# The last two down chunks of the first MLP as one pair, with four of sixteen k tiles in seven products

## The chip, the cores and the metric

The kernel runs on one core of a Trainium2 chip. The metric is the device time of one execution in microseconds, the median of several runs. All times below that are positions ("at 1293") are microseconds from the start of the profiled execution's span.

The core has five engines that work side by side: TensorE (PE; its weight loads are listed as PEld), VectorE (DVE), ScalarE (ACT), GpSimd (POOL) and SyncE (SP). SP computes nothing here; it issues most of the DMA transfers. Each engine works through its own instruction stream in the order that was fixed when the program was built, and waits on semaphores of the others.

## The reference

A decoder trunk of two layers over 256 positions of width 2048, in float32. Each layer is a token mixer (a gated MLP with spatial gating in layer 0, an S5 state-space layer with a gated linear unit in layer 1), then cross-attention to a memory of 256 rows, then a squared-ReLU MLP, each behind an RMSNorm and added to the residual `x`. What matters here is the MLP:

```
def squared_relu_mlp(h, w_up, w_down):
    return jnp.square(jax.nn.relu(h @ w_up)) @ w_down
...
x = x + squared_relu_mlp(rms_norm(x, g_ff[i]), f_w_up[i], f_w_down[i])
```

with `w_up` 2048 x 8192 and `w_down` 8192 x 2048.

## The kernel before

**Arithmetic.** TensorE works on `F32R` operands. Every operand is split into a high part (ACT casts it to F32R) and a low part (DVE subtracts the high part from the raw value): `split`, L103 and L104. A product is then three matmuls: activation high and low with weight high, and activation high with weight low. A weight tile is 512 KB, two k tiles of 128 rows by 512 columns. `wload` loads it on SP into a ring of four raw buffers (`wraw`; the first MLP has a fifth), `wtile` splits it into `whi` and `wlo`, rings of three.

**The first MLP** (`mlp`, layer 0) runs over four blocks `b` of 2048 hidden features. In each block the up products come first: four chunks `n` of 512 features, each as two `gemm_feat` calls, whose results are squared-ReLUed (`r`) and split into `hh` and `hl`. Then come the down products: four chunks `n` of 512 output columns, each a `gemm_hid` of eight weight tiles with 12 matmuls each (two row tiles `t`, two k tiles, three matmuls), added into `x` by `gather` (L688, scaled with the squared norm factor `r2`). In the last block, chunk `n` of `x` is then final, and one tick after it (a tick is one weight tile) `nxt.chunk(x, n)` makes the next layer's activation of it: sums of squares on ACT, eight transposes on TensorE, and high and low parts on ACT (L245) and DVE (L246). The next layer is the S5 mixer, whose first products take the activation's k tiles in order.

**Activations** live in the pool `act` with two slots of 32 KB per partition, tag "act". During the first MLP one slot holds the MLP's own input `hT`, the other the tile `room` of `ssm_prep`. The next activation (`nxt.start()`, `n_b.act` here) takes a slot that is free by then. A tile that takes a slot waits until everything that used the tile before it there has ended.

**`ssm_prep`** prepares the S5 layer's tables beside the first MLP. Its steps are queued in `side` and one is traced at every second tick, at a priority 200 instructions later than its place. It works on small tiles out of `room` and copies them to DRAM on POOL's queue: `Qd`, `Pd` and `Kd`. The last of these copies are four of `Kd` (`respond`, L1191).

**`gemm_seven`** is used by both attentions (values and output projection) and by most of the second MLP, and not by the first MLP. It makes two chunks of 512 columns at once, for both row tiles. For the first k tiles it replaces the eight block products of the 2 x 2 x 2 block scheme by seven, in Strassen's manner: some products take sums of activation blocks (`sums`, made by `token_sums` in four additions and a split, L720 to L723) and differences of raw weight tiles (`run`, L821, L827, L834, L841). Each of the seven is 6 matmuls with its own split of its weights. Four raw tiles are loaded for this by `fetch` (L764) into tiles that `ws()` returns, outside the weight ring. The other weight tiles go through `direct`, 12 matmuls each as in `gemm_hid`, and lie between the products:

```
summed((0, 1), 0, run, t1)
block((1, 0), 0, 0, raw[0, 0], far.get((0, 0)))
m5, m1 = keep((0, 1), 0), keep((1, 0), 1)
block((0, 0), 0, 1, raw[1, 0], far.get((1, 0)))
whole(1, 1)
```

`keep` copies a partial result from PSUM to SBUF (ACT, L812); `gather` then adds it to `x`. With `ahead=None` four of the 16 k tiles go this way; with `ahead`, in the second MLP, eight.

Of the kernel before, what the change touches and what calls it, by code (L numbers as in the profile page):

```python
# [9 lines left out]
F32 = mybir.dt.float32  # L10
F32R = mybir.dt.float32r
# [5 lines left out]
P = 128  # L17
D = 2048
S = 256
KT = D // P  # L20
NB = 512
NCH = D // NB
KB = 2
# [6 lines left out]
DFF = 4 * D  # L30
# [8 lines left out]
class Trunk:  # L39
# [604 lines left out]
    def mlp(self, x, layer, cur, nxt):  # L644
        nc, a, tc = self.nc, self.a, self.tc
        wu, wd = a["f_w_up"][layer], a["f_w_down"][layer]
        hT = cur.act
        with tc.tile_pool(name="ml", bufs=4, reuse_waits="tile") as mp:
            r2 = mp.tile([P, 32 if layer else 24], F32, name="r2", bufs=1)[:, 0:2]
            ws = lambda: mp.tile([P, KB * NB], F32, name="ws", bufs=4)  # L650
            run = lambda: mp.tile([P, KB * NB], F32, name="run", bufs=1)
            kept = lambda i: more[:, 6 + i // 2, i % 2 * NB:i % 2 * NB + NB]
            self.fifth = None if nxt.closing else mp
            for b in range(DFF // D):
                hid = []
                for n in range(NCH):
                    h = mp.tile([P, 4, S], F32R, name="hh")
                    l = mp.tile([P, 4, S], F32R, name="hl")
                    rs = []
                    for i in range(2):  # L660
                        r = mp.tile([P, 2, S], F32, name="r", bufs=2)
                        self.gemm_feat(hT, wu, 2 * (NCH * b + n) + i, r)
                        nc.vector.scalar_tensor_tensor(out=r, in0=r, scalar=0.0, in1=r, op0=ALU.max, op1=ALU.mult)
                        self.split(h[:, 2 * i:2 * i + 2], l[:, 2 * i:2 * i + 2], r)
                        rs.append(r)
                    hid.append((h, l))
                    if nxt.closing and n == 0:
                        sums = []
                    if nxt.closing and n < 2:
                        sums.append(self.token_sums(ws(), lambda: mp.tile([P, 4, 2, P], F32R, name="sums", bufs=4), *rs))  # L670
                    if nxt.closing and n == NCH - 2:
                        more = self.act.tile([P, 8, KB * NB], F32, name="more", tag="act")
                        ahead = [self.block_ahead(more, wd, 2 * j, b * KT, j) for j in range(1 if b == DFF // D - 1 else 2)]
                        ahead[0][-2]()
                if nxt.closing:
                    ahead[0][-1](0, 1, 2)
                if nxt.closing:
                    own = lambda: mp.tile([P, KB * NB], F32R, name="own", bufs=2)
                    nxt.room = lambda: mp.tile([P, 2, NB], F32, name="g", tag="ws", bufs=4)
                if b == 0:  # L680
                    rstd = cur.rstd()
                    nc.vector.tensor_tensor(out=r2, in0=rstd, in1=rstd, op=ALU.mult)
                if b == DFF // D - 1 and not nxt.closing:
                    nxt.start()

                def gather(t, n, part, cs=None):
                    xc = x[:, t, cs or slice(n * NB, (n + 1) * NB)]
                    nc.vector.scalar_tensor_tensor(out=xc, in0=part, scalar=r2[:, t:t + 1], in1=xc,  # L688
                                                   op0=ALU.mult, op1=ALU.add)

                for n in range(NCH):
                    end = b == DFF // D - 1
                    if nxt.closing and not (end and n >= NCH - 2):
                        if n % 2 == 0:
                            self.gemm_seven((ws, run, kept), lambda kt, t: [f[:, kt % 4, t * P:(t + 1) * P]
                                                                            for f in hid[kt // 4]],
                                            sums, wd, n, b * KT, gather, own=own, ahead=ahead[n // 2],
                                            then=ahead[1] if n == 0 and len(ahead) > 1 else None)
                            if end:
                                nxt.start()  # L700
                    elif nxt.closing and end and n == NCH - 1:
                        self.gemm_last(hid, wd, n, b * KT, lambda t, acc: nxt.finish(x, t, lambda cs: gather(
                            t, n, acc[:, cs.start - n * NB:cs.stop - n * NB], cs)))
                        break
                    else:
                        acc = self.gemm_hid(hid, wd, n, b * KT)
                        for t in range(2):
                            gather(t, n, acc[:, t, :])
                    if end:
                        self.at(4 + n if nxt.closing and n < 2 else 1, lambda n=n: nxt.chunk(x, n))  # L710

            self.fifth = None

# [255 lines left out]
    def ssm_prep(self, pool):  # L969
# [28 lines left out]
        def home(n):  # L998
            used[0] += n
            return room[:, used[0] - n:used[0]]  # L1000

        bbs = [home(4 * 2 * 16).rearrange("p (g k c) -> p g k c", g=4, k=2) for _ in range(4)]
        qts = [home((T + 1) * 4 * 16).rearrange("p (w g c) -> p w g c", g=4, c=16) for _ in range(4)]
        pos = [home(4 * 2 * 64).rearrange("p (t r s) -> p t r s", t=4, r=2) for _ in range(4)]
        kds = [home(NL * 2 * 16).rearrange("p (w i c) -> p w i c", i=2, c=16) for _ in range(2)]

        def cmul(orr, oi, ar, ai, br, bi):
            t1 = pool.tile(W, F32, name="cm_1", tag="w4")[:, 0:ar.shape[1]]
            t2 = pool.tile(W, F32, name="cm_2", tag="w6")[:, 0:ar.shape[1]]
            v.tensor_tensor(out=t1, in0=ar, in1=br, op=ALU.mult)  # L1010
            v.tensor_tensor(out=t2, in0=ai, in1=bi, op=ALU.mult)
            v.tensor_tensor(out=orr, in0=t1, in1=t2, op=ALU.subtract)
            v.tensor_tensor(out=t1, in0=ar, in1=bi, op=ALU.mult)
            v.tensor_tensor(out=t2, in0=ai, in1=br, op=ALU.mult)
            v.tensor_tensor(out=oi, in0=t1, in1=t2, op=ALU.add)
# [41 lines left out]
        def zoh():  # L1057
            lr, li = e["lr"], e["li"]
            pr, pi = e["pw"][1]
            fr, fi = pool.tile(W, F32, name="fr", tag="w2"), pool.tile(W, F32, name="fi", tag="w3")  # L1060
            nr, den = pool.tile(W, F32, name="nr", tag="w7"), pool.tile(W, F32, name="den", tag="w9")
            v.tensor_tensor(out=den, in0=lr, in1=lr, op=ALU.mult)
            v.tensor_tensor(out=nr, in0=li, in1=li, op=ALU.mult)
            v.tensor_tensor(out=den, in0=den, in1=nr, op=ALU.add)
            v.reciprocal(out=den, in_=den)
            v.tensor_scalar(out=nr, in0=pr, scalar1=-1.0, scalar2=None, op0=ALU.add)
            v.tensor_scalar(out=li, in0=li, scalar1=-1.0, scalar2=None, op0=ALU.mult)
            cmul(fr, fi, nr, pi, lr, li)
            v.tensor_tensor(out=fr, in0=fr, in1=den, op=ALU.mult)
            v.tensor_tensor(out=fi, in0=fi, in1=den, op=ALU.mult)  # L1070
            pt = self.ps([P, 4, P])
            for k, t in enumerate((fr, fi)):
                nc.tensor.transpose(pt[:, k, :], t, self.ident)
            nc.scalar.copy(out=F, in_=pt[:, 0:2, :])
            e["f"] = fr[:, 0:64], fi[:, 0:64]
            lk = pool.tile([P, 2, 64], F32, name="lk")
            for k in range(2):
                nc.scalar.copy(out=lk[:, k], in_=e["f"][k])
            nc.gpsimd.dma_start(out=Ld[0], in_=lk)
            row(1)  # L1080

        def row(k):
            lk = pool.tile([P, 2, 64], F32, name="lk")
            cmul(lk[:, 0], lk[:, 1], *(f[:, 0:64] for f in e["pw"][k]), *e["f"])
            nc.gpsimd.dma_start(out=Ld[k], in_=lk)

        def power(k):
            h = k // 2
            cmul(*place(k), *e["pw"][h], *e["pw"][k - h])
            if k < T:  # L1090
                row(k)
# [542 lines left out]
```

## Time and profile before

| | us |
|---|---|
| median of 3 runs (2771.16 to 2774.17) | 2772.53 |
| the profiled execution's own time | 2768.95 |
| its span | 2767.2 |
| last block of the first MLP, down products | 1293.6 to 1384.1 |

The span goes from the first to the last instruction. Busy times of engines are the page's first part; stretches of the span can be asked for one by one, with the busy time of each engine in them. A row of a timeline gives the start, the duration, the engine, the line of the kernel, the operation, what it writes and reads, and how many were merged; in brackets stand the idle time before it and what ended it. In a row of a group, `x46` is a count, and three numbers with strokes are minimum, median and maximum in ns. DMA rows have the size and the microseconds from issue to landing.

### The profile page before, as it was taken

The numbers are of one execution on the slowest core, as the hardware profiler recorded it, in microseconds if no ns is written. First come the engines' busy times: TensorE is split into PE (matmuls) and PEld (weight loads), VectorE is DVE, ScalarE is ACT, GpSimd is POOL, SyncE is SP. The second block draws the span as 40 slices with busy tenths as digits, with TensorE's granted clock in tenths as the row PEclk, the third lists the DMA queues.
The fourth block names the chain that finished last, engine by engine and source line by source line (L and its number), as shares of the span: only waits on it lengthen the run. The fifth ranks groups of instructions, "written<-read, shape, count | busy, mean of one in ns | idle before, by whom it ended". The sixth has DMA issues, their size and how long they took to land. (4 is left out here: it accounts for less than half of the span.)

```text
span 2767.2 us, 39486 instructions
## 1 busy us (share of the span) xinstructions
PE 2747.1 (99%) x14978; PEld 2326.5 (84%) x14978; DVE 2046.0 (74%) x2809; ACT 1421.1 (51%) x1814; POOL 186.7 (7%) x331
## 2 busy tenths in 40 slices
PE   9999999999999999999999999999999999999998
PEld 7888888888888888888888888888888888888887
DVE  6865756778888878787577667557767978869685
ACT  6545544555544434444566445445555655546454
POOL 0100000001011111111203100000000000000000
PEclk9999999999999999999999999999999999999999
DMA  8766665557788888886879767565557557475565
GB/s 298 231 196 230 202 183 181 170 159 231 220 281 258 262 258 256 266 256 221 235 238 288 214 202 231 182 195 153 182 163 232 176 174 244 153 248 163 177 212 159
DMA packets 194175, 593.75 MB, mean 215 GB/s; under 512 B 44096, under 2 KB 45168, under 8 KB 193472
## 3 DMA queue, kind: packets, MB, share of 16 engines
q1 hardware_dynamic: 153456, 537.46, 61.3%
q0 software_dynamic: 40000, 52.71, 6.8%
q8 instruction: 117, 1.92, 0.3%
q10 hardware_dynamic: 528, 1.06, 0.1%
q14 instruction: 74, 0.61, 0.1%
HBM read 567.51 MB, written 23.46 MB: 214 GB/s over the span
## 5 line engine op out<-in xcount | busy, mean ns | idle before, releaser
L104 DVE TENSOR_TENSOR wlo<-wraw,whi 128x1024 fp32r<-128x1024 f32 (+1 forms) x865 | 1051.3, 1221 | 444.5 <-ACT whi L103 438.2
L103 ACT CAST whi<-wraw 128x1024 fp32r<-128x1024 f32 (+1 forms) x865 | 909.2, 1053 | 812.2 <-PE acc L875 181.2
L174 PE MATMUL acc<-act,whi 128*128 128x512 f32 x3072 | 740.9, 391 | 0.6 <-DVE act L246 0.6
L174 PEld LDWEIGHTS acc<-act,whi 128*128 128x128 f32 x3072 | 563.1, 188 | 110.7 <-issue 1.4
L179 PEld LDWEIGHTS acc<-act,wlo 128*128 128x128 f32 x3072 | 395.0, 191 | 17.0 <-DVE wlo L104 1.4
L179 PE MATMUL acc<-act,wlo 128*128 128x256 f32 x3072 | 403.2, 283 | 1.2 <-DVE wlo L104 0.8
L159 PE MATMUL acc<-whi,act 128*128 128x512 f32 x1472 | 369.4, 393 | 5.4 <-ACT whi L103 5.4
L159 PEld LDWEIGHTS acc<-whi,act 128*128 128x128 f32 x1472 | 274.8, 189 | 62.6 <-ACT whi L103 5.6
L776 PE MATMUL acc<-whi,act 128*128 128x512 f32 x864 | 233.0, 392 | 0.1
L875 PE MATMUL acc<-whi,hl 128*128 128x512 f32 x544 | 212.7, 391 | 0.0
L874 PE MATMUL acc<-whi,hh 128*128 128x512 f32 x544 | 212.6, 391 | 0.0
L159 PE MATMUL acc<-wlo,act 128*128 128x512 f32 x736 | 197.2, 389 | 0.0
L776 PEld LDWEIGHTS acc<-whi,act 128*128 128x128 f32 x864 | 160.3, 188 | 36.8 <-ACT ends L812 1.9
L159 PEld LDWEIGHTS acc<-wlo,act 128*128 128x128 f32 x736 | 138.3, 188 | 28.9
L877 PE MATMUL acc<-wlo,hh 128*128 128x512 f32 x544 | 145.8, 389 | 0.0
L776 PE MATMUL acc<-wlo,act 128*128 128x512 f32 x432 | 133.1, 390 | 0.0
L190 ACT COPY r<-acc 128x512 f32<-128x512 f32 x64 | 37.7, 589 | 162.9 <-PE acc L174 162.8
L875 PEld LDWEIGHTS acc<-whi,hl 128*128 128x128 f32 x544 | 102.1, 188 | 22.2 <-issue 1.0
L776 PE MATMUL acc<-whi,hh 128*128 128x512 f32 x308 | 120.5, 391 | 0.0
L874 PEld LDWEIGHTS acc<-whi,hh 128*128 128x128 f32 x544 | 102.1, 188 | 21.4 <-issue 0.2
L877 PEld LDWEIGHTS acc<-wlo,hh 128*128 128x128 f32 x544 | 102.0, 188 | 21.4 <-issue 0.2
L776 PE MATMUL acc<-whi,hl 128*128 128x512 f32 x308 | 119.9, 389 | 0.0
(373 smaller groups left out, 2883.5 us busy)
## 6 DMA issues: line engine op xcount, KB each, us to landing
wraw<-in_f_w_up SPq DMA_DIRECT2D x256, 512.0 KB, 4.4
wraw<-in_f_w_down SPq DMA_DIRECT2D x200, 512.0 KB, 5.0
wraw<-in_x_w_q SPq DMA_DIRECT2D x64, 512.0 KB, 4.3
wraw<-in_x_w_k SPq DMA_DIRECT2D x64, 512.0 KB, 4.4
wraw<-in_b_w_out SPq DMA_DIRECT2D x64, 512.0 KB, 4.5
wraw<-in_a_w_in SPq DMA_DIRECT2D x63, 512.0 KB, 4.5
wraw<-in_x_w_v SPq DMA_DIRECT2D x48, 512.0 KB, 4.4
wraw<-in_x_w_o SPq DMA_DIRECT2D x48, 512.0 KB, 4.4
```

Of the source, the lines that this page charges most:

```text
L103: self.nc.scalar.copy(out=hi, in_=src)
L104: return self.nc.vector.tensor_tensor(out=lo, in0=src, in1=hi.bitcast(F32), op=ALU.subtract).ins
L159: nc.tensor.matmul(out[t], a[:, kt, sl], b[:, kk, :], start=st and a is ah, stop=en)
L174: nc.tensor.matmul(acc[:, f, :], hi[:, kk, sl], both[:, kt].rearrange("p a s -> p (a s)"), start=first and kk == 0, stop=last and kk == FK ...
L179: nc.tensor.matmul(acc[:, f, 0:S], lo[:, kk, sl], ah[:, kt, :], start=False, stop=last and kk == FK - 1, skip_group_check=True)
L190: nc.scalar.copy(out=dst, in_=acc[:, :, S:])
L776: mm = lambda s, m, e: nc.tensor.matmul(out, s, m, start=key not in begun, stop=e, skip_group_check=True)
L874: nc.tensor.matmul(acc[:, t, :], ah, hi[:, kk, :], start=kt == 0, stop=False)
L875: nc.tensor.matmul(acc[:, t, :], al, hi[:, kk, :], start=False, stop=False)
L877: nc.tensor.matmul(acc[:, t, :], hid[kt // 4][0][:, kt % 4, sl], lo[:, kk, :], start=False, stop=kt == KT - 1)
```

## The change

In the last block of the first MLP the down chunks n = 2 and n = 3 are made by one call of `gemm_seven` without `ahead`: four of the 16 k tiles in seven products, twelve directly. The token sums that it needs come from the up products of chunk 0 of that block. Their intermediate result is written to a new part of `room` (`self.spare`), their high and low parts to two new tiles `sums`. The four raw weight tiles, the differences (`run`) and the kept results lie in a tile `more`, which is taken from the pool `act` behind the last up products and ahead of the next activation. Chunk 3 of the next activation is planned one tick after chunk 2, both behind the pair. The tile `lk` of `ssm_prep` shares its slot with the tiles of tag `w9`.

```diff
-            ws = lambda: mp.tile([P, KB * NB], F32, name="ws", bufs=4)
-            run = lambda: mp.tile([P, KB * NB], F32, name="run", bufs=1)
+            if nxt.closing:
+                ws = lambda: mp.tile([P, KB * NB], F32, name="ws", bufs=4)
+                run = lambda: mp.tile([P, KB * NB], F32, name="run", bufs=1)
+            else:
+                ws, run = lambda: next(homes), lambda: more[:, 4]
...
-                    if nxt.closing and n == 0:
+                    if n == 0:
                         sums = []
-                    if nxt.closing and n < 2:
-                        sums.append(self.token_sums(ws(), lambda: mp.tile([P, 4, 2, P], F32R, name="sums", bufs=4), *rs))
+                    if nxt.closing and n < 2 or not nxt.closing and n == 0 and b == DFF // D - 1:
+                        sums.append(self.token_sums(ws() if nxt.closing else self.spare, lambda: mp.tile([P, 4, 2, P], F32R, name="sums", bufs=4 if nxt.closing else 2),
+                                                    *rs))
...
                 if b == DFF // D - 1 and not nxt.closing:
+                    more = self.act.tile([P, 8, KB * NB], F32, name="more", tag="act")
+                    homes = iter([more[:, k] for k in range(4)])
                     nxt.start()
...
+                    elif end and n >= NCH - 2 and not nxt.closing:
+                        if n % 2 == 0:
+                            self.gemm_seven((ws, run, kept), lambda kt, t: [f[:, kt % 4, t * P:(t + 1) * P]
+                                                                            for f in hid[kt // 4]],
+                                            sums, wd, n, b * KT, gather)
                     else:
                         acc = self.gemm_hid(hid, wd, n, b * KT)
...
                     if end:
-                        self.at(4 + n if nxt.closing and n < 2 else 1, lambda n=n: nxt.chunk(x, n))
+                        self.at(4 + n if nxt.closing and n < 2 else 1 if n < 3 else 2, lambda n=n: nxt.chunk(x, n))
...
+        self.spare = home(KB * NB)
...
-            lk = pool.tile([P, 2, 64], F32, name="lk")
+            lk = pool.tile([P, 2, 64], F32, name="lk", tag="w9")
```

The last replacement stands twice, in `zoh` and in `row`.

More of the change, by code (lines that the diff above doesn't have):

```diff
@@ L1082, in row @@
         def row(k):
-            lk = pool.tile([P, 2, 64], F32, name="lk")
+            lk = pool.tile([P, 2, 64], F32, name="lk", tag="w9")
             cmul(lk[:, 0], lk[:, 1], *(f[:, 0:64] for f in e["pw"][k]), *e["f"])
```

## Prediction

> **What bounds the kernel now.** I read the page's first two parts first, then the stretches of the stage that changes, then who waits for whom.
>
> ```profile
> span 2767.2 us, 39486 instructions
> PE 2747.1 (99%) x14978; PEld 2326.5 (84%) x14978; DVE 2046.0 (74%) x2809; ACT 1421.1 (51%) x1814; POOL 186.7 (7%) x331
> 617.00:1293.00 676.00, 675.37 (x3665) 573.04 (x3665) 566.23 (x962) 307.50 (x365) 111.07 (x190) 1.00 0.81 251
> 614.76:659.08 44.32, 44.32 (x204) 36.46 (x202) 39.53 (x85) 24.93 (x32) 5.71 (x13) 1.00 0.54 177
> 1338.82:1384.13 45.31, 45.31 (x209) 37.69 (x208) 25.57 (x28) 22.79 (x33) 6.33 (x11) 1.00 0.81 224
> ```
>
> The last three rows are stretches: length, then busy time of PE, weight loads, DVE, ACT, POOL, then the granted clock, the DMA share and GB/s. 1338.82 to 1384.13 is the stage that the change rewrites: the last two down chunks of the first MLP, n = 2 and n = 3. TensorE has no gap in it, at full clock; DVE works 25.57 of 45.31 us, ACT 22.79. So this stage takes as long as its matmuls take to issue. 614.76 to 659.08 is the last pair of the first attention's output projection, which already runs in the form that the change brings. Its ends, the ends of the changed stage and the pace of a tile are these rows of the PE timeline (start, duration):
>
> ```profile
> 614.76 1.08 PE L776 MATMUL acc<-whi,sums 128*128 128x512 f32 x4
> 659.08 1.98 PE L174 MATMUL acc<-act,whi 128*128 128x512 f32 x8
> 1300.82 1.07 PE L877 MATMUL acc<-wlo,hh 128*128 128x512 f32 x4
> 1303.54 0.84 PE L877 MATMUL acc<-wlo,hh 128*128 128x512 f32 x3
> 1383.23 1.07 PE L877 MATMUL acc<-wlo,hh 128*128 128x512 f32 x4
> 1384.13 1.30 PE L159 MATMUL acc<-whi,act 128*128 128x512 f32 x5
> ```
>
> A matmul's own duration overlaps its neighbour's and is not its price; the distance between starts is. From 1300.82 to 1303.54 one weight tile passes, 12 matmuls: 2.72 us, 0.227 us each.
>
> **The matmuls.** Two chunks of eight weight tiles are 2 x 8 x 12 = 192 matmuls. The pair takes four of the tiles (two k steps of each chunk) as seven products of 6 matmuls instead of eight: 42, and the other twelve directly, 144: 186 in all. Six fewer, 6 x 0.227 = **1.36 us** at most. The direct comparison is smaller: both quoted stretches hold two chunks' worth of products and 16 transposes of an activation chunk (eight per chunk, chunks 0 and 1 in the attention, 1 and 2 here), and they take 44.32 and 45.31 us. The new form is **0.99 us** shorter. The second attention's last pair starts at 2024.03 and ends at 2068.37, 44.34 us, so this is no accident of one place.
>
> ```profile
> 2024.03 1.08 PE L776 MATMUL acc<-whi,sums 128*128 128x512 f32 x4
> 2068.37 1.98 PE L174 MATMUL acc<-act,whi 128*128 128x512 f32 x8
> ```
>
> I take 0.99; the ends are 0.97 and 1.36.
>
> **What DVE and ACT get.** Prices from the groups of the tiles `ws` and `more` (min/median/max ns):
>
> ```profile
> L821 DVE TENSOR_TENSOR run<-ws x15: 1212/1221/1227, 465.3 to 2656.0; 128x1024 f32<-128x1024 f32 x15
> L104 DVE TENSOR_TENSOR wlo<-ws,whi x46: 1215/1221/1227, 470.1 to 2676.2; 128x1024 fp32r<-128x1024 f32 x46
> L103 ACT CAST whi<-ws x46: 1031/1051/1058, 468.3 to 2675.1; 128x1024 fp32r<-128x1024 f32 x46
> L812 ACT COPY more<-acc x28: 572/583/591, 2166.1 to 2692.3; 128x512 f32<-128x512 f32 x28
> L688 DVE SCALAR_TENSOR_TENSOR x<-more,r,x x21: 743/745/752, 2169.9 to 2694.8; 128x512 f32<-128x512 f32 x21
> L849 DVE TENSOR_TENSOR more<-more x7: 681/684/687, 2181.4 to 2694.1; 128x512 f32<-128x512 f32 x7
> ```
>
> Seven splits instead of four, four subtractions between raw tiles, three more gathers, one addition: DVE 3 x 1.22 + 4 x 1.22 + 3 x 0.745 + 0.68 = 11.5 us; ACT 3 x 1.05 + 4 x 0.58 = 5.5 us. In the stage DVE goes from 25.6 to about 37 us, ACT to 28. They lie beside the matmuls: in the attention's pair DVE has 39.53 of 44.32 us and TensorE still has no gap. Without that cover the price would be 1.08 us (2.44 of DVE against 1.36 of matmul) for each of the four products whose weights are subtracted first, 4.3 us; I take 0, and keep 4.3.
>
> The token sums come once, in the up products of chunk n = 0 of the last block: four operations of 0.42 us and a split, 4 x 0.42 + 1.22 = 2.9 us of DVE, 1.05 of ACT. That is in the first stretch above, where DVE is busy 566.23 of 676 us and TensorE still misses only 0.63. 16% of DVE is free there and weights are split two tiles ahead, so I take 0; the bound is 2.9.
>
> ```profile
> L722 DVE TENSOR_TENSOR ws<-r x8: 414/416/418, 2087.2 to 2621.8; 128x256 f32<-128x256 f32 x8
> ```
>
> **What moves: loads.** Four loads of 512 KB go into the slot that the up products leave and no longer wait for the weight ring, so SP can issue them from about 1293, together, ahead of ring loads. The same burst stands in the second MLP:
>
> ```profile
> 2121.53 2.74 SPq L737 DMA_DIRECT2D more<-in_f_w_down x4
> wraw<-in_f_w_down SPq DMA_DIRECT2D x200, 512.0 KB, 5.0
> 1293.00:1318.00 25.00, 25.00 (x125) 20.29 (x124) 13.56 (x16) 11.56 (x14) 1.01 (x2) 1.00 0.63 196
> 1329.00:1335.00 6.00, 6.00 (x29) 4.95 (x28) 3.03 (x3) 2.11 (x2) 1.23 (x3) 1.00 1.05 360
> ```
>
> TensorE waits for nothing near 2121. From 1293 to 1318 the DMA engines are 0.63 busy, and 2 MB more in those 25 us are 80 GB/s on top of 196; at 1329, where they would have no room, these bytes are gone. I take 0.
>
> **What moves: activation slots.** There are two. Now the raw tiles take the one that the up products leave, so the next stage's activation (`n_b.act`) gets the other, which `ssm_prep`'s `room` holds until its last copies to DRAM have landed. Before, its first write (chunk 0, ACT at L245) had nothing to wait for. Rows of the ACT and POOL timelines, with the landing of the last four copies and of all 64:
>
> ```profile
> 1319.79 0.82 ACT L245 ACTIVATE act<-ps,gcol 128x256 fp32r<-128x256 f32 x2
> 1316.99 2.27 POOL L1191 DMA_DIRECT2D Kd<-room x4 [33.47 <-ACT room L1183]
> DMA to landing us min/median/max: 2.0/3.4/3.7
> DMA to landing us min/median/max: 2.0/5.1/6.9
> 1301.02 1.06 ACT L103 CAST whi<-wraw 128x1024 fp32r<-128x1024 f32 x1 [1.62 <-PE acc L875]
> ```
>
> The last copy is issued at about 1318.7 and lands by 1318.7 + 3.7 = 1322.4: the write at 1319.79 comes 2.6 us too early. Behind it on ACT stand the casts of the next weight tiles, and DVE's low halves and TensorE wait for those. How far ahead are they? The cast at 1301.02 starts when the first eight matmuls of a tile end (1300.82, above), and is for the third tile on: ready at 1302.08, needed once four matmuls and two tiles have passed, at 1300.82 + 4 x 0.227 + 2 x 2.72 = 1307.17. That is **5.1 us** of cover, more than 2.6. Cost 0. Were the copies to take the 6.9 us of the slowest of all 64, ACT would be held 5.8 us and TensorE 0.7.
>
> **What moves: the end.** The features of chunk 2 used to be made beside n = 3; now those of chunks 2 and 3 are both made behind the pair, beside the first products of the S5 layer. The 16 transposes are as many as before. The next product needs chunk 2 after four tiles (4 x 2.72 = 10.9 us) and chunk 3 after six (16.3). Where the same tail stands before the second MLP, whose first product asks for all 16 k tiles sooner, TensorE's whole wait list shows
>
> ```profile
> PE acc L174 <- DVE act L246: 0.6, 1, 0.6
> PE acc L179 <- ACT act L245: 0.3, 1, 0.3
> ```
>
> so the bounds are 0 and 0.9 us; I take 0, since the deadlines here are later. The tile `lk` that shares a slot with `den` is still written in turn with its own copies, as before: 0.
>
> **Sum.** On the profiled execution (span 2767.2, its own time 2768.95): -0.99 + 0. That execution is 3.6 us under the median of the runs shown, 2772.53, to which I apply the same difference: 2772.53 - 1.0 = **2771.5 us**. What a measurement of this kernel can tell from no change is about 0.2%, 5.5 us: the forecast is no measurable difference.
>
> **Rivals.**
> 1. *The seven products are bound by DVE.* For: 2.44 us of DVE for 1.36 us of matmul. Against: the attention's pair. It gives 2772.53 - 1.0 + 4.3 = 2775.8, within 0.2%. Chance 0.10.
> 2. *ACT is held at `n_b.act` (slower).* Place: the write of chunk 0, behind the last copies from `room`. TensorE loses from 5.1 us of hold on; the kernel is slower by 0.2% once the loss exceeds 5.5 + 1.0, a hold of 11.6 us, that is, once the last copy lands later than 1331.4, 12.7 us after its issue. For: other transfers of the same queue in this stretch land that late:
>
> ```profile
> dq<-Kd POOLq DMA_DIRECT2D x2, 128.0 KB, 16.4
> ```
>
> At 16.4 us the hold would be 15.3, the loss 10.2, and the time 2781.7. Against: these copies are issued ahead of those transfers, took at most 3.7 us, and the write may simply stand later in ACT's order. Chance 0.07. [...] No row of before shows ACT at such a wait. [...]
> 3. *The slots fall the other way*, the raw tiles into `room`'s and `n_b.act` where it was. The loads then wait until 1322.4, 16 us ahead of the pair's first product, and land in some 5: the time is the forecast's, 2771.5. Chance 0.08.
> 4. *Faster by over 0.2%.* TensorE would have to save 5.5 us; the matmuls hold 1.36 and the stage no gap. Only a lucky reordering later is left. Chance 0.04.
>
> **Chances.** Forecast 0.68, rival 1 0.10, rival 2 0.07, rival 3 0.08, rival 4 0.04; 0.03 for a slower cause that I don't see. Within 0.2%: 0.68 + 0.10 + 0.08 = 0.86; slower 0.07 + 0.03 = 0.10; faster 0.04. The range takes in the spread of the runs (2771.16 to 2774.17, about 1.5 us each way) around 2771.5, down to the lower end of the matmul saving and a low median, 2768.5, and up to rival 1, 2776.5; it leaves out rivals 2 and 4.
>
> **What would show it.** Right: 186 matmuls and no gap in the pair, 44.3 us with 16 transposes or 43.4 with chunk 1's eight alone; DVE near 37 us; the first L245 of `n_b.act` at 1322 to 1326 with no TensorE wait behind it. Wrong: TensorE waiting for `wlo` or `whi` in the pair (rival 1) or just behind 1325 (rival 2); a `wlo` wait near 1210 to 1230 (the sums); a wait for `act` within 16 us after the pair (the end); a `wraw` wait after 1293 (the burst).

## The result, and the profile after

The changed kernel takes 2777.47 us (median of 10 runs, 2774.85 to 2782.32); the kernel before, measured beside it, 2771.36 (10 runs, 2766.98 to 2775.9). The ratio is 1.0023, 95% interval 1.0015 to 1.003: **6.1 us slower**, where 1.0 us less was forecast, and above the range given. The profiled execution took 2782.32 us, the slowest of its runs. By 301 us it is already 2.2 us behind the profile of before, far ahead of the stage that changes; a second profile of the same kernel (shown below) is 0.3 us behind there, so this belongs to the execution and not to the change. Positions in it are about 2.2 us later than those of before, and stages are compared by their lengths.

The page of the changed kernel, span and busy times (engine, us, share of the span, instructions):

```profile
span 2780.6 us, 39485 instructions
PE 2753.2 (99%) x14972; PEld 2328.7 (84%) x14972; DVE 2057.8 (74%) x2825; ACT 1423.9 (51%) x1822; POOL 186.3 (7%) x331
```

Six matmuls fewer than before (14978), as the change says, and still 99% busy: the averages hide what happened. The list of who waited for whom does not; TensorE's part of it from 1293 to 1400 (waited in total, times, longest), empty in the same stretch of before, reads now:

```profile
PE acc L787 <- DVE wlo L104: 2.5, 1, 2.5
PE acc L888 <- DVE wlo L104: 2.1, 1, 2.1
PE acc L787 <- ACT junk L198: 0.2, 1, 0.2
```

Stretches of the changed kernel (length, busy PE, PEld, DVE, ACT, POOL, granted clock, DMA share, GB/s):

```profile
1341.00:1356.00 15.00, 11.01 (x27) 7.97 (x28) 11.64 (x13) 8.06 (x12) 4.10 (x7) 0.66 0.86 200
...
1361.00:1392.00 31.00, 30.94 (x136) 25.07 (x135) 18.78 (x18) 14.16 (x16) 1.15 (x2) 1.00 0.53 171
```

In the first 15 us TensorE starts 27 matmuls where 15 / 0.227 = 66 would fit. It is idle for 4 us of them (the first gap begins just ahead, at 1340.3), and the granted clock is 0.66. From 1361 on, everything is as in the stage before: full clock, no gap. The loss lies in one place, the entry into the pair. Rows of the timeline of the changed kernel there, all engines (start, duration, engine, line, operation, in brackets the idle time ahead of it and what ended it):

```profile
1277.78 48.87 SPq L127 DMA_DIRECT2D wraw<-in_f_w_down  x18
...
1319.18 2.26 POOL L1203 DMA_DIRECT2D Kd<-room  x4 [33.47 <-ACT room L1195]
...
1321.98 0.82 ACT L245 ACTIVATE act<-ps,gcol 128x256 fp32r<-128x256 f32 x2
...
1324.45 2.22 POOL L1251 DMA_DIRECT2D pq<-Pd  x4
1326.60 2.49 POOL L1251 DMA_DIRECT2D dq<-Kd  x4
1327.00 3.20 SPq L775 DMA_DIRECT2D more<-in_f_w_down  x4
...
1339.91 1.22 DVE L832 TENSOR_TENSOR more<-more 128x1024 f32<-128x1024 f32 x1 [8.13 <-DMA more<-in_f_w_down]
1341.05 1.22 DVE L104 TENSOR_TENSOR wlo<-wraw,whi 128x1024 fp32r<-128x1024 f32 x1
...
1342.33 1.93 PE L888 MATMUL acc<-wlo,hh 128*128 128x512 f32 x4 [2.06 <-DVE wlo L104]
...
1346.32 1.23 DVE L845 TENSOR_TENSOR more<-more 128x1024 f32<-128x1024 f32 x1 [2.49 <-DMA more<-in_f_w_down]
...
1349.87 1.22 PE L787 MATMUL acc<-wlo,hh 128*128 128x512 f32 x2 [2.47 <-DVE wlo L104]
```

This is to be read from the bottom up. TensorE waits for `wlo` at 1342.33: a low half of the last direct tile, which has nothing to do with the raw tiles. DVE made it late, at 1341.05, because ahead of it in DVE's order stands L832, the first subtraction of raw tiles, and that waited 8.13 us for its data. The second gap has the same cause with L845. The raw tiles were late because SP issued their loads only at 1327.00, behind 18 loads of the weight ring, and not at 1293. And the reason for that is in the row of 1321.98: the first write of `n_b.act` comes at the same place of the stage as before (there 1319.79), with no wait. The last copy out of `room` is issued at 1320.9 and no copy of this group lands in under 2.0 us (2.0 to 6.8 over its 64), so this write cannot have waited for `room`. So `n_b.act` has the slot that the up products leave, and the raw tiles have `room`'s, free only behind the copies of 1319.18. The slots fell the other way than I took it. The reading, which the first experiment tests, is that a slot goes to the tile whose first use comes first: chunk 0 of the activation is written before the pair asks for its loads.

From the DMA view of the changed kernel, 1326 to 1352 (busy tenths of 16 DMA engines in 40 slices; issues with count, size and median us to landing):

```profile
DMA  7797899999999999999999999999999999999553
wraw<-in_f_w_down SPq DMA_DIRECT2D x4, 512.0 KB, 9.4
more<-in_f_w_down SPq DMA_DIRECT2D x4, 512.0 KB, 14.2
```

The loads left into full DMA engines: at 1324 and 1326 POOL issued the S5 stage's own first loads, `pq` and `dq`. The raw tiles took 14.2 us to landing (the trace gives the landing of one of the four), where the median load of `w_down` into the ring took 5.0 over the whole kernel before.

### The profile page after: what moved, and what is told of

It is laid out like the page before. It is cut to its first block, busy times and chain, and to the rows that moved or that the text cites. A ratio compares the mean times of both kernels' runs of the same rounds, so it can differ in the third digit from the quotient of the medians.

```text
span 2780.6 us, 39485 instructions
## 1 busy us (share of the span) xinstructions
PE 2753.2 (99%) x14972; PEld 2328.7 (84%) x14972; DVE 2057.8 (74%) x2825; ACT 1423.9 (51%) x1822; POOL 186.3 (7%) x331
## 5 line engine op out<-in xcount | busy, mean ns | idle before, releaser
L888 PE MATMUL acc<-wlo,hh 128*128 128x512 f32 x480 | 129.5, 391 | 2.1 <-DVE wlo L104 2.1
L787 PE MATMUL acc<-wlo,hh 128*128 128x512 f32 x362 | 112.8, 393 | 2.5 <-DVE wlo L104 2.5
L888 PEld LDWEIGHTS acc<-wlo,hh 128*128 128x128 f32 x480 | 90.3, 188 | 21.5 <-DVE wlo L104 2.5
L886 PEld LDWEIGHTS acc<-whi,hl 128*128 128x128 f32 x480 | 90.1, 188 | 19.7 <-issue 1.0
```

The lines of the kernel that those rows point to most:

```text
L787: mm = lambda s, m, e: nc.tensor.matmul(out, s, m, start=key not in begun, stop=e, skip_group_check=True)
L886: nc.tensor.matmul(acc[:, t, :], al, hi[:, kk, :], start=False, stop=False)
L888: nc.tensor.matmul(acc[:, t, :], hid[kt // 4][0][:, kt % 4, sl], lo[:, kk, :], start=False, stop=kt == KT - 1)
```

## Experiments

**Theory A**: slot and full DMA engines make the raw tiles late; DVE, in order, holds the low halves behind them; TensorE gets two gaps, and a slow clock behind them. **Theory B**: the seven products themselves cost time in this place (DVE's 11.5 us). **Theory C**: the hold of ACT at `n_b.act`, rival 2 of the prediction. The length used below is that from the first down product of the last block to the first S5 product, from the PE timelines. It is 90.57 us before (with 24 transposes; chunk 2's eight, 0.79 us, lie behind it in the changed kernel) and 98.84 in the changed one (1295.75 to 1394.59).

### The raw tiles get the slot of the up products

```diff
-                    homes = iter([more[:, k] for k in range(4)])
+                    homes = iter([more[:, k] for k in range(4)]); nc.vector.memset(more[:, 5, 0:1], 0.0)
```

One element is written, so that the first use of `more` comes ahead of that of `n_b.act`. Nothing else is changed.

> The changed kernel with one more instruction: a one-column memset of the tile of raw tiles at the place where it is taken from the pool, so that it is the first of the two new tiles to be used and gets the slot that the up products leave. Theory A (the raw tiles got the slot of the S5 tables, their loads went out only at 1327, into a saturated stretch of DMA, and landed too late): the loads go out by about 1300, TensorE waits for nothing in the pair, and the ratio to before is 0.9985 to 1.0005, some 6 us better than the change. Theory B (the seven products cost more than they save here, whatever the slot): the waits for wlo in the pair stay and the ratio is 1.0015 to 1.003. Theory C (ACT is held at the next activation, which now has the slot of the tables): a wait behind 1322, ratio over 1.001, and the same in the run with the slots swapped alone.

Measured: 2772.02 us (11 runs), ratio 1.0005 [0.9996, 1.0013]. The length is 88.81 us, and TensorE waits for nothing from 1290 to 1400. Its timeline:

```profile
1294.15 1.28 SPq L775 DMA_DIRECT2D more<-in_f_w_down  x2
...
1304.98 0.42 SPq L775 DMA_DIRECT2D more<-in_f_w_down  x1
...
1323.14 0.83 ACT L245 ACTIVATE act<-ps,gcol 128x256 fp32r<-128x256 f32 x2
...
1339.21 1.07 PE L787 MATMUL acc<-whi,sums 128*128 128x512 f32 x4
```

and from its DMA view, 1290 to 1312, its stretches, and the groups of TensorE from 1335 to the end of the pair:

```profile
more<-in_f_w_down SPq DMA_DIRECT2D x4, 512.0 KB, 5.9
```

```profile
1339.40:1382.77 43.37, 43.31 (x195) 35.41 (x194) 30.46 (x32) 23.82 (x32) 5.26 (x9) 1.00 0.61 182
```

```profile
L787 PE MATMUL acc<-whi,hl 128*128 128x512 f32 x54 | 21.0, 390 | 0.0
L787 PE MATMUL acc<-whi,hh 128*128 128x512 f32 x54 | 20.9, 393 | 0.1
L787 PE MATMUL acc<-wlo,hh 128*128 128x512 f32 x54 | 16.6, 389 | 0.0
L787 PE MATMUL acc<-whi,sums 128*128 128x512 f32 x16 | 4.4, 395 | 0.0
L787 PE MATMUL acc<-wlo,sums 128*128 128x512 f32 x8 | 2.5, 390 | 0.0
```

54 + 54 + 54 + 16 + 8 = 186 matmuls at full clock with no gap. The loads are issued from 1294 to 1305 and land in 5.9 us, before 1312; the first product comes at 1339, and the pair takes 43.56 us (1339.21 to 1382.77), where 43.4 was forecast for this case. The pair with the same arithmetic as the changed kernel's costs nothing extra. B falls, and so does C: `n_b.act` now has `room`'s slot, is first written at 1323.14, and nobody waits. The saving is 90.57 - 0.79 - 88.81 = 0.97 us.

### The slot alone, without the pair

The kernel before, with a tile `more` claimed in the same way, which was meant to give `n_b.act` the slot of `room`:

```diff
-                    nxt.start()
+                    more = self.act.tile([P, 8, KB * NB], F32, name="more", tag="act"); nc.vector.memset(more[:, 5, 0:1], 0.0); nxt.start()
```

> The kernel before, whose last two down chunks stay as they were; only the slots are exchanged, by a tile that takes the slot of the up products with a one-column memset. Theories A and B: no change, ratio 0.999 to 1.001, the first write of the next activation at about 1322 instead of 1320, no TensorE wait. Theory C: slower, ratio over 1.001, TensorE waits for whi or wlo between 1320 and 1335.

Measured: 2770.73 us, ratio 1.0 [0.9991, 1.0009], length 90.57 us as before, no wait of TensorE from 1293 to 1400. But the slots were not exchanged. Its timeline:

```profile
1294.25 0.06 DVE L684 MEMSET more<- 128x1 f32 x1 [1.48 <-PE acc L174]
...
1317.34 2.25 POOL L1191 DMA_DIRECT2D Kd<-room  x4 [33.36 <-ACT room L1183]
...
1319.98 0.91 ACT L245 ACTIVATE act<-ps,gcol 128x256 fp32r<-128x256 f32 x2
```

The first write of `n_b.act` comes at 1319.98, not at the 1322 that was expected. The last copy out of `room` is issued at 1319.0, and none of the 64 landed in under 2.0 us in the profiles of before and of the changed kernel, so this write did not wait for it. Nothing but the memset uses `more` here; its slot was free again at once, and `n_b.act` will have taken it. So this run says nothing on C. What is known of C comes from the claimed slot with the pair.

### Late loads, without the S5 loads beside them

The changed kernel, slots as they fell, and the S5 stage's first `pq` and `dq` loads moved from POOL to SP, behind the last weight tiles of the MLP; and, as a control, the kernel before with the same move.

```diff
-                fetch("pq", 0, i)
+                fetch("pq", 0, i, True)
...
-                fetch("dq", 0, i)
+                fetch("dq", 0, i, True)
```

> The changed kernel with the slots as they fell, but the first loads of the S5 tables (pq and dq of its first chunk) go out on SP behind the last down load, so that the stretch from 1322 on is free of them. Theory A: the four raw tiles still go out at about 1327 but land in 5 to 8 us instead of 14, TensorE has no wait in the pair, and the time is 0 to 2 us under that of its control (the kernel before with the same late loads). Theory B: the pair keeps its waits, 5 to 8 us over the control.

> Control: the kernel before with the first loads of the S5 tables on SP behind the last down load. All theories: the stage of the last down chunks stays at 90.6 us; the S5 layer may lose a few us to the later loads, ratio 0.999 to 1.004. It is there to be compared with the changed kernel under the same edit.

Measured: 2800.04 us (ratio 1.011 [1.0094, 1.0125]) and 2804.13 (1.0117 [1.0103, 1.0131]), four runs each. Both pay a new wait at the start of the S5 stage, 28.2 and 27.1 us, because its weights now queue behind the moved loads; for the control a few us had been expected. So the totals say little, and the two intervals overlap; the length, which ends ahead of that wait, says it. The control's is 90.57 us, as before. In the first, from the timeline:

```profile
1325.23 1.91 SPq L775 DMA_DIRECT2D more<-in_f_w_down  x4
...
1331.92 1.23 DVE L832 TENSOR_TENSOR more<-more 128x1024 f32<-128x1024 f32 x1 [1.92 <-DMA more<-in_f_w_down]
```

The loads are issued as late as in the changed kernel, but the first subtraction starts 6.7 us behind them instead of 1339.91 - 1327.00 = 12.9. There is no wait in the pair, and up to the new wait the length is 88.82 us, that of the claimed slot (88.81).

The DMA engines are full in both kernels: their share is 0.94 in these 6.7 us, and 0.99 in the changed kernel from 1327 to 1340. What differs is who has them. Queues in the DMA views (packets, MB, share of the 16 engines; q1 is SP's, q0 is POOL's), the changed kernel from 1327 to 1340 first, then this one from 1325.23 to 1332:

```profile
q1 hardware_dynamic: 599, 2.21, 50.4%
q0 software_dynamic: 895, 2.12, 48.8%
```

```profile
q1 hardware_dynamic: 628, 2.32, 94.2%
```

SP's queue moves in 6.8 us what took it 13 us beside POOL's loads. So neither the late issue nor the seven products alone makes the gaps: it takes the late issue *and* the `pq` and `dq` loads beside it. A high DMA share alone does not: with the claimed slot it is 0.88 from 1294 to 1306, and the tiles land in 5.9 us.

### The changed kernel again, and another order on DVE

The second of these two differs from the changed kernel only in DVE's order: the first subtraction goes behind the last direct tile's low half.

```diff
-        v.tensor_tensor(out=run, in0=raw[0, 1], in1=raw[0, 0], op=ALU.subtract)
+        with self.tc.issue_after(self.low) if first_mlp else nullcontext(): v.tensor_tensor(out=run, in0=raw[0, 1], in1=raw[0, 0], op=ALU.subtract)
```

> The changed kernel once more, beside the others of this call: is its loss the same in a second profile? Theory A (the four raw tiles are issued behind room's last copies, into full DMA engines, land late, and hold DVE and so TensorE): the loads issued at about 1327 again, landing above 10 us, two TensorE waits for wlo of 1.5 to 3 us each between 1340 and 1351, clock below 1 in the ten microseconds behind them, 98 to 100 us from the first down product to the first S5 product, ratio 1.0015 to 1.003. If the gaps were an accident of one execution, they differ by more than a microsecond here or are gone.

> The changed kernel with one difference: the first subtraction of raw tiles is queued on DVE behind the low half of the last direct tile in front of the pair, not ahead of it. The loads stay as late. If the loss is only the place in DVE's order, the wait of 2.1 us at L888 and that of 2.5 us at L787 both go and the time is 2771 to 2772. Theory A, data that come late wherever the subtraction stands: the wait at L888 goes, but the first product still lacks its weights; its own wait grows to between 2.5 and 4.6 us, the clock still falls behind it, the stage takes 94 to 98 us, 2773 to 2777.

Measured: 2777.41 us (ratio 1.0022 [1.0013, 1.0031]) and 2778.25 (1.0024 [1.0015, 1.0033]). Lengths 96.48 and 97.24 us. TensorE's waits from 1293 to 1400, the changed kernel again first, the other order second:

```profile
PE acc L888 <- DVE wlo L104: 2.9, 1, 2.9
PE acc L787 <- ACT junk L198: 0.7, 1, 0.7
PE acc L787 <- DVE wlo L104: 0.2, 1, 0.2
```

```profile
PE acc L787 <- DVE wlo L104: 3.9, 1, 3.9
PE acc L787 <- ACT whi L103: 1.3, 1, 1.3
```

The loss of the changed kernel is no accident of one execution: the loads are late again, with 14.9 us to landing. Its split over the two gaps is: I had expected two waits of 1.5 to 3 us and a length of 98 to 100, and the second execution has one wait of 2.9, two small ones, and 96.48 us. With the other order the direct tile is on time (no wait at L888), and the first product waits all the more, 5.2 us in two pieces, more than the 2.5 to 4.6 expected, and the time is a little above its range too. DVE's order only decides who is hit first. The data are late for the pair itself.

### A gap by itself

In the kernel before, one added DVE addition of 128 x 8192 (or 128 x 6144) into a tile that nothing reads afterwards is queued ahead of the gather that precedes chunk n = 2.

```diff
+                        if end and n == 2:
+                            with tc.issue_after(self.low):
+                                again = [f.rearrange("p k s -> p (k s)").bitcast(F32).unsqueeze(1).broadcast_to([P, 8, KB * NB]) for f in hid[0]]
+                                nc.vector.tensor_tensor(out=more[:, 0:8], in0=again[0], in1=again[1], op=ALU.add)
```

> The kernel before, with one added DVE addition of 128 x 8192 (estimated at 8 x 1.22 = 9.8 us from the groups' 128 x 1024) queued behind a low half ahead of the gather of chunk n = 1; slots, loads and matmuls as before. It makes a gap on TensorE of about the hold less some 5 us of cover, so 3 to 6 us, at a place where nothing else is changed. If a gap costs only itself: the stage from the first down product to the first S5 product is 90.6 plus the gap, and the clock reads 1.00 behind it. If the gap also makes TensorE slow for a while, as the changed kernel's profile suggests (4.8 us of waits, about 5 more of slow clock): the clock falls below 0.7 in the five microseconds behind the gap, the stage is 90.6 plus the gap plus 3 to 7 us, and the time 2776 to 2784.

> The same with 128 x 6144 (7.3 us): a gap of 1 to 3 us, near to each of the two of the changed kernel. If the slow clock depends on the length of the gap, it is shorter than with 8192 or absent, and the time 2771.5 to 2774; if any such gap brings it, the stage is 90.6 plus the gap plus 3 to 7 us, 2775 to 2780.

Measured: 2780.4 us (ratio 1.0033 [1.002, 1.0045]) and 2773.93 (1.0008 [0.9999, 1.0017]). Three things came out otherwise than planned. The operation took 8.68 and 6.55 us, not 9.8 and 7.3. TensorE was covered for longer than the 5 us assumed. So in the first MLP the gaps were smaller than expected: 1.5 us in three pieces, the longest 1.0, and none; the lengths are 92.81 and 90.57. And the condition holds in the second MLP too, whose last block has its own chunk n = 2, so each kernel holds DVE a second time there, at 2712 and 2710. That place turned out to be the useful one. Both medians lie in the ranges expected, but by luck: those were worked out for one gap in the first MLP. The long hold's PE timeline and a stretch:

```profile
2722.31 0.76 PE L878 MATMUL acc<-whi,hh 128*128 128x512 f32 x1 [3.81 <-DVE x L688]
...
2727.56 0.53 PE L878 MATMUL acc<-whi,hh 128*128 128x512 f32 x1
```

```profile
2723.00:2728.00 5.00, 5.00 (x14) 3.90 (x13) 4.62 (x6) 3.79 (x9) 0.00 (x0) 0.51 0.43 134
```

And the short hold's:

```profile
2718.19 0.47 PE L878 MATMUL acc<-whi,hh 128*128 128x512 f32 x1 [1.67 <-DVE x L688]
...
2721.59 0.39 PE L878 MATMUL acc<-whi,hh 128*128 128x512 f32 x1
```

```profile
2721.00:2726.00 5.00, 5.00 (x24) 4.09 (x23) 4.76 (x6) 2.59 (x4) 0.00 (x0) 1.00 0.84 249
```

One gap of 3.81 us, and the next tile of 12 matmuls takes 2727.56 - 2722.31 = 5.25 us instead of 2.72, at half clock, with all its data there: the gap costs 3.81 + 2.5. A gap of 1.67 us leaves the clock at 1.00. The next tile takes 3.40 us there, most of the excess at a second wait of its own (0.66 us between two starts instead of 0.227). So a gap can cost more than itself. When it did, the last section shows.

### The claimed slot once more

The first profile of the claimed slot had a longer S5 stage than before (310.3 us against 306.5). Same kernel, to see whether that belongs to it:

> The changed kernel with the claim once more. In its first profile the stage was 88.8 us, but the S5 stage behind it 310.3, against 306.5 in the profile of before, with one TensorE wait of 2.5 us and a clock of 0.97 in the 50 us around it. If that belongs to the edit (the activation now in room's slot, other places in the queues), the S5 stage is 309 to 311 us again and the time 2771.5 to 2773, no less than before. If it is the accident of one execution, the S5 stage is 306 to 308.7 us, no wait there is above 2 us, the down stage is 88.8 us again, and the median 2769.5 to 2771.5, below or level with before.

Measured: 2771.45 us, ratio 0.9996 [0.9987, 1.0005]; length 88.81 us again; S5 stage 308.67, its longest wait 1.5 us. The S5 stage varies as much without the other slot: it takes 306.98 and 308.30 us in the two profiles of the changed kernel and 308.65 in that of the slot alone, where `n_b.act` lies as before. So 308.67 shows no price of the other slot, and the 310.3 did not come again; that execution holds a gap of 2.53 us, which the last section takes up. The version with the claim is level with the kernel before, and no version measured beats it.

## Why the prediction was wrong

**The step that failed is "What moves: activation slots".** It put it that "the raw tiles take the one that the up products leave", from the order in which the tiles are asked for in the program. The slot goes by first use, and the opposite happened. All that hung on it (issue at about 1293, room for the loads on the DMA engines, "I take 0" for the loads) then spoke of a kernel that was not built; the experiment with the claimed slot is that kernel, and there it came true in the main: issue from 1294.15, though not all together but up to 1304.98, landing in 5.9 us, and no wait.

**Rival 3 was this case, with chance 0.08 and a wrong price.** It said that the loads wait until 1322.4 and "land in some 5". Two terms were off:
- The issue: 1327.00, in positions of before about 1324.8. SP's order puts the loads behind the ring loads of the tiles ahead of them; they left right behind the last of those 18.
- The landing: 14.2 us, not 5. The 5.0 was the median over 200 loads of the whole kernel, while the prediction itself quoted the row of 1329 to 1335 with a DMA share of 1.05 and had used it only to say that the bytes would be gone by then. In rival 3 they were not gone. In the DMA view of before, 1326 to 1352, the ring loads land in 8.3 us and POOL's `dq` loads in 11.9 to 13.8; from there the price would have been open, not 5.

At 5 us the data would have been there by 1332 to 1335, six to nine us ahead of the first product, which was due at 1341 (1339.21 with the claimed slot, where the down products begin 1.8 us earlier). With 14.2 they were not.

**The price of a wait was missing.** Even with the right landing I would have charged the waits alone. In the profiled execution they are 2.06 + 2.47 + 0.19 = 4.7 us. The rest is slow clock: ten matmuls from 1342.33 to 1346.31 take 3.98 us instead of 2.27, and fourteen from 1349.87 to 1356.38 take 6.32 without the wait instead of 3.18, together 4.9 us. 4.7 + 4.9 = 9.6 of the 98.84 - 88.81 = 10.0 us that this stage takes longer than with the claimed slot. In the second profile of the changed kernel it is 96.48 - 88.81 = 7.7 us, with one long gap instead of two. Between medians, each against the kernel before on its own chip, the loss is 6.1 and 6.6 us; against before the stage is longer by 96.48 + 0.79 - 90.57 = 6.7 us in that second profile.

**What was right.** The matmuls: 0.99 us forecast, 0.97 measured. Against rival 1, DVE is no bound: with the claimed slot it works 30.46 us of 43.37, less than the 37 forecast, because three of the four subtractions and two of the seven splits lie ahead of the stretch and chunk 2's features behind it. A reader of the changed kernel's waits alone would have voted for rival 1, since both long ones name `wlo`, its sign in "What would show it". What tells them apart is the bracket in the DVE row: 8.13 us *idle* ahead of L832. Against rival 2: no wait with `n_b.act` in `room`'s slot, first written at 1323.14 and 1322.73 in the two profiles of the claimed slot, where 1322 to 1326 was forecast; without the pair this was not tried. The token sums: from the last row of the attention (659.08 before) to the first down product of the last block pass 634.48 us before and 634.43 in the changed kernel. The end: no TensorE wait between the pair and 1400 in either form.

## What to carry to other kernels

A tile's buffer is settled by who uses it first, not by who asks first: before counting on an early prefetch, find the first use of every tile that competes for the slot, and if the prefetch must win, let it write first. A load that loses its early slot must be priced with the loads of other queues that are in flight at its new place: here it took 14.2 us to landing beside POOL's. A median over the kernel (5.0 before) does not give that price, and the DMA share alone (0.94 without POOL's loads, 0.99 with them) does not either. And TensorE gaps of some 2 us (2.06 and 2.47 here) can cost themselves and a slow stretch behind them (4.9 us here).

## What the runs showed of the hardware

I had not expected the clock to fall after gaps this short. In the eleven profiles TensorE has 27 idle gaps of 0.9 us or more behind the first 200 us. Behind the 17 of 0.92 to 1.85 us the granted clock stays at 1.00. Of the ten from 2.06 us up, nine are followed by a clock near 0.50 (2.06, 2.16, 2.47, 2.53, 2.86, 3.81, 3.87, 27.1 and 28.2 us), and one of 2.79 us is not. So the length alone does not decide.

More can be read from narrow stretches. In the profiles of before and of the changed kernel the record of the granted clock begins and changes only at the marks of a grid of 3.41 us: it begins at 9.12 and changes at 2760.26 in before, 806 such windows later; in the changed kernel it begins at 11.33 and changes at 1342.52 (390 windows later), 1345.94, 1349.35, 1356.18 and 2776.12 (420 windows behind 1342.52). The slow stretches of the changed kernel between the start and the end of its work last 3.41 and 6.83 us, one and two windows; those at the gaps of 27.1 and 28.2 us, in the two profiles with the moved loads, 27.31 us, eight windows. The first five windows around the gaps of the changed kernel:

```profile
1339.11:1342.52 3.41, 1.34 (x7) 0.81 (x6) 2.36 (x2) 0.99 (x2) 0.59 (x1) 1.00 1.04 257
1342.52:1345.94 3.42, 3.42 (x9) 2.64 (x9) 1.23 (x1) 1.94 (x3) 0.59 (x1) 0.50 1.08 251
1345.94:1349.35 3.41, 1.46 (x7) 0.85 (x5) 3.04 (x3) 0.00 (x0) 0.59 (x1) 1.00 1.04 239
1349.35:1352.76 3.41, 2.70 (x6) 1.73 (x7) 3.41 (x5) 2.25 (x6) 1.74 (x3) 0.50 0.56 117
1352.76:1356.18 3.42, 3.42 (x10) 2.65 (x9) 2.87 (x4) 2.87 (x5) 1.18 (x3) 0.50 0.67 171
```

Idle is what a window's length leaves beside the busy PE; the ends of matmuls, and so the idle times, are modelled. A window with 3.41 - 1.34 = 2.07 us of idle TensorE is followed by one at half clock, a busy one by one at full clock, one with 1.95 us idle again by half clock, and a slow one with 0.7 us idle by another slow one. Over all windows of the profiles of before and of the changed kernel, one at full clock is followed by a slow one where TensorE was idle for 1.95 us of it or more, and never where it was idle for 1.81 us or less. A slow window is followed by another where it had 0.70 us idle (that at 1349.35) or more, and by full clock where it had none (those at 1342.52 and 1352.76). What lies between was not met in these two. The exception, in the profile of the long hold, agrees with this:

```profile
1558.46 0.65 PE L1353 MATMUL ps<-dq,us 128*32 128x128 f32 x16 [2.79 <-DMA dq<-Kd]
```

```profile
1553.68:1557.09 3.41, 2.00 (x23) 1.22 (x21) 2.45 (x2) 1.12 (x2) 0.00 (x0) 1.00 0.80 228
1557.09:1560.51 3.42, 2.05 (x81) 1.67 (x82) 0.00 (x0) 0.29 (x1) 0.00 (x0) 1.00 0.90 308
```

A mark at 1557.09 cuts the gap of 2.79 us in two, 1.41 and 1.37 us, and neither window has as much as the 1.81 us that left the clock at 1.00 elsewhere. The gap of 2.53 us, with 2.27 of it in one window, was followed by a slow one. The windows give the price too: at a clock of 0.50, a slow one costs up to half of its 3.41 us. The three slow windows of the changed kernel hold 10.24 us, 0.70 of them idle, and (10.24 - 0.70) / 2 = 4.8 us is what was found above as 4.9.

Three of the ten long gaps, those of 2.16, 2.53 and 2.79 us, lie at the small products of the S5 stage, where gaps differ from execution to execution. The gap of 2.53 us stands at L1369 in the claimed slot's first profile; in its second profile the gap there was 1.5 us, the clock 1.00, and the S5 stage 1.6 us shorter. Part of the spread between runs of one kernel may come from such gaps, now slow behind and now not; that was not tried.
